# Projecting the S5 part of the second half's tiles before the feed-forward, with the last early tile's residual and norm in halves on VectorE

## The chip, the cores and the metric

One of the eight cores of one Trainium2 chip runs the whole program. The metric is device time in microseconds, the median of several executions of the same program. Everything is float32; matrix products run on operands split into a high and a low part (fp32r), three TensorE instructions for each product.

## What is computed

A decoder layer for 1024 positions of width 1024. The part that matters here is the output projection of the mixers and the second sub-layer (cut from the reference):

```python
mix = jnp.concatenate([rms_norm(o_a, out_norm_g[l, :a_end]),
                       rms_norm(o_b, out_norm_g[l, a_end:b_end]),
                       rms_norm(o_c, out_norm_g[l, b_end:])], axis=-1)
x = x + ga1 * (mix @ w_out[l])

h = rms_norm(x, norm2_g[l]) * (1 + sc2) + sh2
x = x + ga2 * (jnp.square(jax.nn.relu(h @ w_ff1[l])) @ w_ff2[l])
```

`o_a` (384 columns) comes from a sliding-window attention, `o_b` (256 columns) from the S5 state-space mixer, `o_c` (384 columns) from the three-branch attention. The rows of `w_out` are therefore eight slabs of 128: slabs 0 to 2 belong to A, 3 and 4 to S5, 5 to 7 to C.

## The kernel before

The 1024 positions are eight tiles of 128. S5 is finished for all tiles early (about a quarter into the span); its normed output lies in DRAM as `mixB_d`. Attention A and C go tile by tile. Tiles 0 to 3 (the first half) are finished first; then the feed-forward of the first half (`feed_forward`, L2153) runs while attention goes through tiles 4 to 7, then the output projection of the second half (`late_proj`, L1806) runs between the last pieces of that feed-forward, and last the feed-forward of the second half (`late_feed_forward`, L2118).

The output projection of one tile for one group of slabs is, for each of two column halves of 512, three TensorE instructions a slab (`mm3`, so 12 instructions of 128x512 a tile for the two S5 slabs, 18 for the three A or C slabs), and one addition into the tile's page `y[n]` (`add_y`, L1516). A and C need a factor of the norm for each row, so `add_y` scales them; S5 is normed before and needs none (`r is None`).

- `early_ab` (L1771) loads slabs 0 to 4, projects A and S5 of tiles 0 to 3 as soon as attention A has left them, then loads slabs 5 to 7 and the gate row `rows_of[2]`.
- `tile_end(n)` (L1792), for n of 0 to 3, projects C, adds the residual (`residual`, L1668: the gate on GpSimd, the addition on VectorE, over all 1024 columns), then the second norm and its transposition (`norm2_steps`, L1683): a square sum on ScalarE, the reciprocal root on GpSimd (`rstd_pool`, L470), the scaling on VectorE, and four `turn` steps of two TensorE transposes each. The first product of `feed_forward` needs tile 3's last `turn` steps.
- `late_proj` loads slabs 0 to 2, then 3 and 4, then 5 to 7, and projects the groups A, S5 and C of tiles 4 to 7 in this order, group after group.
- `load_ff` (L1905) loads a feed-forward weight slab of 512 KB, copies the high part on ScalarE and takes the low part on GpSimd.

The order of all instructions is not the order of the code. The code is run once to record calls; `run_plan` (L405) takes the steps by planned times, and `listed` (L216) then lists the recorded calls on the engines by the planned rank, readiness and its own prices. What comes out is a fixed order on each in-order engine. In the profile all recorded instructions have the line L2191, so groups are told apart by tile names: `pa` and `pb` are the eight banks of PSUM, `b` the pages of 1024, `u` those of up to 804, `s` of 384, `small` the columns of statistics, `wide` the identity of a transpose.

## Time and profile before

| | |
|---|---|
| median of 3 runs | 1365.98 us (1362.07 to 1370.18) |
| the profiled execution's own time | 1368.67 us |
| its span in the trace | 1367.0 us |
| mean granted TensorE clock | 0.973 |
| TensorE busy | 1306.1 us (96%) |
| VectorE busy | 954.8 us (70%) |
| ScalarE busy | 749.3 us (55%) |
| GpSimd busy | 639.1 us (47%) |

Shares of busy time are averages over stages that have different limits; the tables by stretch and the timelines below say what each stage is limited by. A granted clock of 1.00 is 2.4 GHz, of 0.50 is 1.2 GHz; a value between is a mean over a stretch that had both.

### The profile page before, as it was taken

What the parts mean: (1) busy time and instruction counts of PE and PEld (TensorE: products, weight loads), DVE (VectorE), ACT (ScalarE), POOL (GpSimd) and SP (SyncE); (2) the same over time, 40 slices, a digit from 0 to 9 for tenths busy, and PEclk for the clock granted to TensorE, in tenths of its full rate; (3) what the DMA queues carried; (4) which work ended last, traced back from release to release, by engine and by line L of the source; (5) the groups of instructions that cost most, each with busy time, mean ns of one, the idle gap of its engine ahead of it and who ended that gap; (6) DMA issues with size and microseconds to landing.
All of it is one profiled execution on the core that took longest, in us unless ns stands there. A gap on an engine that the chain in (4) does not pass through costs nothing.

```text
span 1367.0 us, 19734 instructions
## 1 busy us (share of the span) xinstructions
PE 1306.1 (96%) x6862; PEld 1115.3 (82%) x6862; DVE 954.8 (70%) x1979; ACT 749.3 (55%) x1657; POOL 639.1 (47%) x604
## 2 busy tenths in 40 slices
PE   5998998998999869999999999999999999999998
PEld 4898998997787558888888888888787888888886
DVE  7868977787788545465565576463558887788896
ACT  6445367567666775565565565542354445544450
POOL 3477734034567365455465465575553233122230
PEclk9999999999899789999999999999999999999999
DMA  9445436223122222212222343244464432323221
GB/s 364 177 141 170 153 117 214 95 72 116 39 76 108 89 89 69 74 64 68 95 80 62 119 144 120 75 143 146 153 223 162 155 123 78 107 94 108 78 93 62
DMA packets 59570, 161.03 MB, mean 118 GB/s; under 512 B 6447, under 2 KB 22349, under 8 KB 59469
## 3 DMA queue, kind: packets, MB, share of 16 engines
q1 hardware_dynamic: 51661, 145.86, 32.3%
q10 hardware_dynamic: 7808, 13.91, 2.7%
q8 instruction: 54, 0.88, 0.3%
q14 instruction: 47, 0.39, 0.1%
HBM read 140.59 MB, written 19.14 MB: 117 GB/s over the span
## 4 chain that ended last, share of the span: by engine, by line
PE 76%; DVE 7%; ACT 3%; issue 2%; POOL 1%; DMA 1%; ACTq 0%; DVEq 0%; SPq 0%; POOLq 0%
PE pb L2191 41%; PE pa L2191 35%; DVE b L2191 4%; ACT b L2191 2%; DVE pb L2191 1%; ACT u L2191 1%; POOL b L2191 1%; DMA mixB_d<-b 1%; DVE k L2191 1%; DVE small L2191 0%; DVE u L2191 0%; DVE s L2191 0%; DMA b<-in_ada_dram 0%; ACT s L2191 0%; ACT k L2191 0%
## 5 line engine op out<-in xcount | busy, mean ns | idle before, releaser
L2191 PE MATMUL pb<-b,b 128*128 128x512 f32 (+2 forms) x2478 | 590.2, 385 | 1.4 <-DVE b L2191 1.3
L2191 PEld LDWEIGHTS pb<-b,b 128*128 128x128 f32 (+1 forms) x2478 | 446.0, 190 | 85.7 <-DVE b L2191 2.8
L2191 POOL TENSOR_TENSOR b<-b,b 128x1024 fp32r<-128x1024 f32 (+6 forms) x140 | 322.7, 2312 | 293.2 <-ACT b L2191 188.0
L2191 PE MATMUL pa<-b,b 128*128 128x512 f32 (+2 forms) x1830 | 364.3, 349 | 9.5 <-ACT b L2191 4.4
L2191 PEld LDWEIGHTS pa<-b,b 128*128 128x128 f32 (+1 forms) x1830 | 291.7, 195 | 49.8 <-ACT b L2191 5.3
L2191 ACT ACTIVATE b<-b 128x1024 fp32r<-128x1024 f32 (+4 forms) x266 | 242.0, 927 | 100.8 <-DMA b<-in_ff_dram 42.6
L2191 DVE TENSOR_TENSOR b<-b,b 128x1024 fp32r<-128x1024 f32 (+4 forms) x181 | 200.2, 1136 | 21.8 <-ACT b L2191 12.1
L2191 PE MATMUL pa<-u,b 128*128 128x384 f32 (+2 forms) x836 | 202.0, 364 | 7.4 <-DVE small L2191 2.0
L2191 PEld LDWEIGHTS pa<-u,b 128*128 128x128 f32 x836 | 148.3, 206 | 16.2 <-ACT u L2191 4.6
L2191 DVE TENSOR_TENSOR b<-pa,b 128x512 f32<-128x512 f32 (+2 forms) x168 | 107.6, 650 | 65.3 <-PE pa L2191 61.8
L2191 ACT ACTIVATE u<-pa 128x384 fp32r<-128x384 f32 (+4 forms) x205 | 97.1, 478 | 84.3 <-PE pa L2191 83.3
L2191 DVE TENSOR_TENSOR u<-pa,u 128x384 fp32r<-128x384 f32 (+1 forms) x173 | 94.9, 553 | 55.7 <-ACT u L2191 55.2
L2191 DVE TENSOR_TENSOR b<-pb,b 128x512 f32<-128x512 f32 (+2 forms) x120 | 76.2, 647 | 60.1 <-PE pb L2191 55.2
L2191 POOL TENSOR_SCALAR b<-b,small 128x64 f32<-128x64 f32 (+8 forms) x118 | 75.2, 648 | 68.9 <-DVE small L2191 55.8
L2191 PE MATMUL pa<-wide,b 128*128 128x128 f32 (+1 forms) x443 | 81.7, 296 | 24.8 <-DVE b L2191 19.1
L2191 POOL TENSOR_SCALAR u<-u,small 128x256 f32<-128x256 f32 (+3 forms) x90 | 55.1, 623 | 100.0 <-DVE small L2191 78.4
L2191 PEld LDWEIGHTS pa<-wide,b 128*128 128x128 f32 (+1 forms) x443 | 58.4, 149 | 43.5 <-DVE b L2191 21.2
L2191 POOL TENSOR_TENSOR b<-r,b 128x512 fp32r<-128x512 f32 x37 | 51.2, 1383 | 80.6 <-ACT b L2191 80.1
L2191 ACT ACTIVATE b<-pb 128x512 f32<-128x512 f32 (+3 forms) x60 | 29.1, 509 | 87.0 <-PE pb L2191 72.4
L2191 ACT ACTIVATE u<-pb,small 128x256 f32<-128x256 f32 (+6 forms) x126 | 60.2, 485 | 28.7 <-DVE small L2191 28.0
L2191 ACT ACTIVATE b<-pb,small 128x64 f32<-128x64 f32 (+4 forms) x130 | 62.5, 493 | 20.4 <-DVE small L2191 15.6
L2191 PE MATMUL pb<-k,u 128*128 128x320 f32 (+10 forms) x300 | 70.0, 344 | 2.3 <-ACT b L2191 2.1
(145 smaller groups left out, 1446.2 us busy)
## 6 DMA issues: line engine op xcount, KB each, us to landing
b<-in_ff_dram SPq DMA_DIRECT2D x128, 512.0 KB, 3.6
b<-in_ada_dram SPq DMA_DIRECT2D x48, 512.0 KB, 6.0
b<-in_x_dram SPq DMA_DIRECT2D x16, 512.0 KB, 7.1
b<-in_wo_dram SPq DMA_DIRECT2D x16, 512.0 KB, 4.3
r<-in_w_in_dram SPq DMA_DIRECT2D x16, 256.0 KB, 2.6
b<-in_cw_dram SPq DMA_DIRECT2D x8, 512.0 KB, 5.4
x_d<-b ACTq DMA_DIRECT2D x8, 512.0 KB, 3.2
out_dram<-b SPq DMA_DIRECT2D x16, 256.0 KB, 2.2
```

What stands on the lines that cost most here:

```text
L2191: method(*args, **kw)
```

## The change

1. In `early_ab`, after the last slabs are loaded, the S5 group of tiles 4, 5 and 6 is projected and the pages go to a new DRAM tensor `yB_d`, through ScalarE's queue. Tile 7's is projected in `tile_end(3)`. `add_y` copies the first S5 half instead of scaling it.
2. `late_proj` has two groups of slabs, A and C. It loads the pages from `yB_d` on SyncE's queue and adds to them. The loads and splits of slabs 3 and 4, and the four loads of `mixB_d`, go from there.
3. For tile 3 alone `half_residual` takes the place of `residual`: gate and addition on VectorE in halves of 512 columns, each followed by its square sum on ScalarE; the norm adds the two sums on VectorE and scales in halves.
4. The low parts of the first four feed-forward weight slabs of the first half are taken on VectorE instead of GpSimd.

```diff
@@ add_y
-            ts(d, o, r, ALU.mult)
+            if r is None:
+                V.tensor_copy(out=d, in_=o)
+            else:
+                ts(d, o, r, ALU.mult)
@@ new
+    def half_residual(n, i):
+        c = slice(i * 512, i * 512 + 512)
+        if not i:
+            normed[n] = page(1024)
+        tt(y[n][:, c], y[n][:, c], rows_of[2][:, c], ALU.mult)
+        tt(x2[n][:, c], x2[n][:, c], y[n][:, c], ALU.add)
+        A.activation(out=normed[n][:, c], in_=x2[n][:, c], func=AF.Square, accum_out=ss4[:, i:i + 1])
+        if i:
+            nc.scalar.dma_start(out=x2_d[n], in_=x2[n])
@@ norm2_steps, scale
+            if t in normed:
+                h = normed[t]
+                tt(ss2[:, t:t + 1], ss4[:, 0:1], ss4[:, 1:2], ALU.add)
+                rstd_pool(rs2[:, t:t + 1], ss2[:, t:t + 1], 1, D)
+                for c in (slice(0, 512), slice(512, 1024)):
+                    ts(h[:, c], x2[t][:, c], rs2[:, t:t + 1], ALU.mult)
@@ early_ab, behind load_row(2)
+        for n in range(NT // 2, NT - 1):
+            steps = proj_steps(n, [3, 4], load_b(n))
+            for f in steps:
+                f()
+                yield 6.0 / len(steps)
+            nc.scalar.dma_start(out=yB_d[n - 4], in_=y.pop(n))
@@ tile_end
-        for f in proj_steps(n, [5, 6, 7], st) + [lambda: residual(n)] + norm2_steps(n):
+        steps = proj_steps(n, [5, 6, 7], st)
+        if n == 3:
+            for i in range(2):
+                steps.insert(2 * i + 1, lambda i=i: half_residual(n, i))
+            steps += proj_steps(7, [3, 4], load_b(7)) + [lambda: nc.scalar.dma_start(out=yB_d[3], in_=y.pop(7))]
+        else:
+            steps.append(lambda: residual(n))
+        steps += norm2_steps(n)
+        for f in steps:
@@ late_proj
-        late, tiles, groups = {}, range(4, NT), ((0, 1, 2), (3, 4), (5, 6, 7), ())
+        late, tiles, groups = {}, range(4, NT), ((0, 1, 2), (5, 6, 7), ())
-                if i == 1:
-                    late[n] = load_b(n)
-                    continue
+                if not i:
+                    y[n] = page(1024)
+                    nc.sync.dma_start(out=y[n], in_=yB_d[n - 4])
@@ load_ff
-        split_lo(G, lo, raw, hi)
+        split_lo(V if not half and kind == 1 and i < 4 else G, lo, raw, hi)
```

How the change moves instructions shows at three places.

TensorE, behind the C projection of tile 3 (the last product of it is the first row; `b314,u608` and `b314,u617` are score products of the next attention unit; `wide,b612` and `wide,b622` are tile 3's norm transposes; `b418,u620` to `b422,u620` are tile 7's S5 group; `u610` and `u621` are attention weights). Before:

```order
L2191 MATMUL pa2_65<-b548_629,b606_687 128x512
L2191 MATMUL pb0_67<-b314_395,u608_689 128x256 x4
L2191 MATMUL pb1_68<-b314_395,u608_689 128x256 x2
L2191 MATMUL pa1_64<-wide_91,b612_693 128x128
L2191 MATMUL pa2_65<-wide_91,b612_693 128x128
...
L2191 MATMUL pa1_64<-wide_91,u610_691 128x128 x3
L2191 MATMUL pa2_65<-wide_91,q611_692 128x128 x3
L2191 MATMUL pb2_69<-b571_652,b619_700 128x512
```

After:

```order
L2229 MATMUL pa2_65<-b548_630,b615_697 128x512
L2229 MATMUL pb0_67<-b314_396,u617_699 128x256 x3
L2229 MATMUL pb1_68<-b314_396,u617_699 128x256 x2
L2229 MATMUL pa1_64<-b418_500,u620_702 128x512
...
L2229 MATMUL pa2_65<-b422_504,u620_702 128x512
L2229 MATMUL pa1_64<-wide_91,u621_703 128x128 x3
L2229 MATMUL pa3_66<-u626_708,b275_357 128x384
L2229 MATMUL pa2_65<-wide_91,q623_705 128x128 x3
...
L2229 MATMUL pa2_65<-wide_91,b622_704 128x128
```

Twelve products of tile 7's S5 group, and then transposes, value and score products of the attention, stand between the score products and tile 3's transposes, where before nothing stood.

VectorE, the same place (`b517` is tile 3's page `y`, `b609` and `b618` its residual, `b612` and `b622` its normed page, `b624` tile 7's page, `b636` and `b639` low parts of feed-forward slabs). Before:

```order
L2191 SCALAR_TENSOR_TENSOR b517_598<-pa1_64,small_71,b517_598 128x512
L2191 SCALAR_TENSOR_TENSOR b517_598<-pa2_65,small_71,b517_598 128x512
L2191 ISA pb0_67,small_71<-pb0_67,u322_403,small_71 128x256
...
L2191 TENSOR_REDUCE small_71<-small_71 128x3
L2191 TENSOR_TENSOR b609_690<-b609_690,b517_598 128x1024
L2191 RECIPROCAL small_71<-small_71 128x3
L2191 TENSOR_SCALAR b612_693<-b609_690,small_71 128x1024
```

After:

```order
L2229 SCALAR_TENSOR_TENSOR b517_599<-pa1_64,small_71,b517_599 128x512
L2229 TENSOR_TENSOR b636_718<-b634_716,b635_717 128x1024
L2229 TENSOR_TENSOR b517_599<-b517_599,b556_638 128x512
L2229 SCALAR_TENSOR_TENSOR b517_599<-pa2_65,small_71,b517_599 128x512
L2229 TENSOR_TENSOR b618_700<-b618_700,b517_599 128x512
L2229 TENSOR_TENSOR b517_599<-b517_599,b556_638 128x512
L2229 COPY b624_706<-pa1_64 128x512
L2229 TENSOR_TENSOR b618_700<-b618_700,b517_599 128x512
...
L2229 COPY b624_706<-pa2_65 128x512
L2229 TENSOR_TENSOR u626_708<-pa1_64,u626_708 128x384
L2229 TENSOR_TENSOR small_71<-small_71 128x1
L2229 TENSOR_TENSOR b639_721<-b637_719,b638_720 128x1024
...
L2229 TENSOR_SCALAR b622_704<-b618_700,small_71 128x512
```

Gate, addition and scaling of tile 3 stand in halves on VectorE, with two low parts, the two copies of tile 7's page and attention splits between them; the rows left out are the score maxima, as before, and two more attention splits.

TensorE in the late projection, between the A group and the C group (`u1083`, `u1099` are the last A tile; in the first fence `u1099` of slabs `b1087` is the first S5 tile; `ones` are the norm sums of the C group; `u1114` is the first C tile). Before:

```order
L2191 MATMUL pa2_65<-b1071_1152,u1083_1164 128x512
L2191 MATMUL pb0_67<-b574_655,b1056_1137 128x512
...
L2191 MATMUL pa3_66<-b1087_1168,u1099_1180 128x512
...
L2191 MATMUL pb2_69<-b1094_1175,u1099_1180 128x512
L2191 MATMUL pb3_70<-b1060_1141,b1040_1121 128x512
```

After:

```order
L2229 MATMUL pa2_65<-b1081_1163,u1099_1181 128x512
L2229 MATMUL pb0_67<-b574_656,b1068_1150 128x512
...
L2229 MATMUL pa0_63<-ones_92,s1115_1197 128x1 x3
...
L2229 MATMUL pb0_67<-b576_658,b1069_1151 128x512
L2229 MATMUL pa1_64<-ones_92,s1124_1206 128x1 x3
L2229 MATMUL pa3_66<-b1102_1184,u1114_1196 128x512
```

Before, the S5 group follows the A group, in turn with feed-forward products; now the C group follows after one feed-forward unit's eighteen products and the four norm sums.

The S5 group of tile 4 now stands on both sides of the C projections of tiles 0 and 1, in two pieces of six products; those of tiles 5 and 6 stand further on among attention and norm transposes of tiles 1 to 3, in two pieces of six each as well.

## Rows read from the trace of the kernel before

**Rows 1.** The page, part 4: the chain that ended last, by engine.
```profile
PE 76%; DVE 7%; ACT 3%; issue 2%; POOL 1%; DMA 1%; ACTq 0%; DVEq 0%; SPq 0%; POOLq 0%
```

**Rows 2.** Busy time by stretch; columns: us, then busy us and count of each engine, granted clock.
```profile
900.00:1000.00 100.00, 99.42 (x473) 81.81 (x473) 54.87 (x75) 38.22 (x61) 58.14 (x49) 1.00 0.42 138
```

**Rows 3.** Busy time by stretch around the long gap, columns as in Rows 2.
```profile
429.80:441.00 11.20, 10.43 (x61) 8.70 (x60) 10.72 (x34) 8.40 (x28) 10.36 (x13) 1.00 0.39 141
441.00:456.00 15.00, 11.61 (x47) 6.44 (x45) 10.12 (x26) 14.57 (x41) 7.83 (x8) 0.80 0.21 72
456.00:472.20 16.20, 12.92 (x63) 9.84 (x63) 9.67 (x23) 11.48 (x27) 3.93 (x4) 0.82 0.14 45
472.20:479.70 7.50, 7.49 (x24) 5.91 (x24) 2.82 (x7) 1.94 (x8) 3.72 (x4) 0.66 0.67 199
...
489.20:500.00 10.80, 10.16 (x47) 8.29 (x48) 4.36 (x14) 9.24 (x24) 4.68 (x3) 0.76 0.37 116
```

**Rows 4.** Timeline of TensorE, 432 to 493 us: start, us, operation, [idle before <-releaser].
```profile
432.85 2.23 PE L2191 MATMUL pa<-b,b 128*128 128x512 f32 x9
...
472.18 6.80 PE L2191 MATMUL pa<-b,b 128*128 128x512 f32 x18 [0.54 <-ACT b L2191]
478.81 0.88 PE L2191 MATMUL pb<-b,u 128*128 128x256 f32 x6
489.21 0.69 PE L2191 MATMUL pa<-wide,b 128*128 128x128 f32 x2 [9.52 <-DVE b L2191]
...
492.52 1.20 PE L2191 MATMUL pb<-b,b 128*128 128x512 f32 x2
```

**Rows 5.** Timeline of VectorE, 479 to 489 us.
```profile
479.01 0.75 DVE L2191 SCALAR_TENSOR_TENSOR b<-pa,small,b 128x512 f32<-128x512 f32 x1 [1.77 <-PE pa L2191]
479.68 0.48 DVE L2191 CUSTOM_DVE_ANT_1 pb<-pb,u,small 128x256 f32<-128x256 f32 x1
...
482.90 1.23 DVE L2191 TENSOR_TENSOR b<-b,b 128x1024 f32<-128x1024 f32 x1
...
488.18 0.98 DVE L2191 TENSOR_SCALAR b<-b,small 128x1024 f32<-128x1024 f32 x1 [3.97 <-POOL small L2191]
```

**Rows 6.** Timeline of GpSimd, 479 to 489 us.
```profile
479.84 2.34 POOL L2191 TENSOR_TENSOR b<-b,b 128x1024 f32<-128x1024 f32 x1 [1.38 <-DVE b L2191]
483.81 2.52 POOL L2191 TENSOR_TENSOR b<-b,b 128x1024 fp32r<-128x1024 f32 x1 [1.62 <-ACT b L2191]
...
486.87 0.19 POOL L2191 TENSOR_SCALAR small<-small 128x1 f32<-128x1 f32 x1
...
487.60 0.55 POOL L2191 TENSOR_TENSOR small<-small 128x1 f32<-128x1 f32 x1
```

**Rows 7.** Timeline of TensorE, 932 to 954 us.
```profile
932.75 1.56 PE L2191 MATMUL pa<-b,u 128*128 128x512 f32 x6
934.15 1.57 PE L2191 MATMUL pb<-b,u 128*128 128x512 f32 x6
...
953.40 2.34 PE L2191 MATMUL pa<-b,u 128*128 128x512 f32 x9
```

**Rows 8.** Timelines of SyncE's queue and of GpSimd, 925 to 944 us.
```profile
925.31 5.89 SPq L2191 DMA_DIRECT2D b<-in_wo_dram  x3
...
936.21 7.14 POOL L2191 TENSOR_TENSOR b<-b,b 128x1024 fp32r<-128x1024 f32 x3
```

**Rows 9.** Groups of VectorE instructions by shape: count, busy us, mean ns, idle before.
```profile
L2191 DVE TENSOR_TENSOR u<-pa,u 128x384 fp32r<-128x384 f32 x157 | 86.2, 554 | 51.9 <-ACT u L2191 51.3
...
L2191 DVE COPY b<-pa 128x512 f32<-128x512 f32 x14 | 9.3, 687 | 7.7 <-issue 4.9 <-PE pa L2191 2.8
```

**Rows 10.** Timelines of VectorE and of GpSimd, 461 to 466 us.
```profile
461.60 0.41 DVE L2191 TENSOR_TENSOR b<-b,b 128x256 fp32r<-128x256 f32 x1
...
464.07 1.35 DVE L2191 TENSOR_TENSOR b<-b,b 128x256 fp32r<-128x256 f32 x1
...
462.77 2.37 POOL L2191 TENSOR_TENSOR b<-b,b 128x1024 fp32r<-128x1024 f32 x1 [10.76 <-ACT b L2191]
```

More of the change, by code (lines that the diff above doesn't have):

```diff
@@ L30 @@
 SLOTS = dict(k=(1088, 4), b=(1024, 38), u=(804, 10), r=(804, 2), s=(384, 5), q=(384, 1))
-SMALL = 1288
+SMALL = 1292
 TC = dict(schedule_with_timeline_sim=True)
@@ L1672, in residual @@
         nc.scalar.dma_start(out=x2_d[n], in_=x2[n])
+    normed = {}
+    def half_residual(n, i):
[7 more added lines that the diff above has]
+            nc.scalar.dma_start(out=x2_d[n], in_=x2[n])
     def load_row(v):
@@ L1680, in trunk @@
     h2l = [None, None]
-    ss2, rs2 = cols(8), cols(8)
+    ss2, rs2, ss4 = cols(8), cols(8), cols(3)
     def norm2_steps(t):
@@ L1690, in scale @@
                 h2l[hf] = [page(1024) for _ in range(4)]
-            h = page(1024)
-            A.activation(out=h, in_=x2[t], func=AF.Square, accum_out=ss2[:, t:t + 1])
-            rstd_pool(rs2[:, t:t + 1], ss2[:, t:t + 1], 1, D)
-            ts(h, x2[t], rs2[:, t:t + 1], ALU.mult)
+            if t in normed:
[5 more added lines that the diff above has]
+            else:
+                h = page(1024)
+                A.activation(out=h, in_=x2[t], func=AF.Square, accum_out=ss2[:, t:t + 1])
+                rstd_pool(rs2[:, t:t + 1], ss2[:, t:t + 1], 1, D)
+                ts(h, x2[t], rs2[:, t:t + 1], ALU.mult)
             hold.append(h)
@@ L1734, in trunk @@
     oC_d = dr.tile([4, 128, 384], F32, name="oC_d")
+    yB_d = dr.tile([4, 128, 1024], F32, name="yB_d")
     def a_phase():
@@ L1800, in tile_end @@
         load_x2(n)
-        for f in proj_steps(n, [5, 6, 7], st) + [lambda: residual(n)] + norm2_steps(n):
+        steps = proj_steps(n, [5, 6, 7], st)
[3 more added lines that the diff above has]
+            steps += proj_steps(7, [3, 4], load_b(7)) + [lambda: nc.scalar.dma_start(out=yB_d[3], in_=y.pop(7))]
+        else:
+            steps.append(lambda: residual(n))
+        steps += norm2_steps(n)
+        for f in steps:
             f()
@@ L1811, in late_proj @@
             yield L_PACE
-        for i, fs in enumerate(groups[:3]):
+        for i, fs in enumerate(groups[:2]):
             for n in tiles:
                 yield L_PACE
-                if i == 1:
-                    late[n] = load_b(n)
-                    continue
+                if not i:
+                    y[n] = page(1024)
+                    nc.sync.dma_start(out=y[n], in_=yB_d[n - 4])
                 o, late[n] = load_o(oC_d[n - 4] if i else oA_d[n]), []
```

## Prediction

> **What bounds the kernel now.** I read the chain of waits first: three quarters of it lie on TensorE, 7% on VectorE, little elsewhere [rows 1]. So the question for every part of the change is whether it takes TensorE work off a stretch where TensorE is full, or fills a stretch where it waits. The table of busy time by stretch answers that. From 500 us to the end of the late projection TensorE has next to no idle time: 99.42 us of the 100 from 900 to 1000, at the full clock [rows 2]. Around 430 to 500 us it looks otherwise: TensorE is busy 11.61 of 15.0 us and 12.92 of 16.2 us there, its granted clock is 0.80 and 0.82, and 0.66 in the last C projection [rows 3]. The timeline shows why the end of this stage is worst: after tile 3's C projection (18 products from 472.18) and six score products, TensorE does nothing for 9.52 us and then starts tile 3's transposes at 489.21; the first feed-forward product follows at 492.52 [rows 4]. What it waits for is a chain over three engines. VectorE adds the second half at 479.01 [rows 5]; GpSimd applies the gate, 2.34 us; VectorE adds the residual, 1.23 us; ScalarE sums squares; GpSimd is then busy with a feed-forward low part (2.52 us from 483.81) before it takes the root, 486.87 to 488.15 [rows 6]; VectorE scales from 488.18 [rows 5]. Everything behind 492.52 is TensorE at its limit, so a microsecond taken before that point, or a product taken out behind it, comes off the end.
>
> **Late projection: out.** The S5 group of tiles 4 to 7 is 4 tiles x 2 halves x 2 slabs x 3 = 48 products of 128x512. In the timeline, groups of six start 1.40 us apart (932.75, 934.15), 0.233 us a product [rows 7], so 48 x 0.233 = 11.2 us leave a full TensorE. VectorE's eight additions go with them, and two slab loads with their splits; TensorE does not wait for these there, so they count nothing. What may come back: slabs 5 to 7 are requested from 925.31 and GpSimd ends their low parts at 943.35 [rows 8], 18.0 us later, while the C group starts only at 953.40 [rows 7], with the S5 group between. In the new order only eighteen feed-forward products and the norm sums stand between A and C, about 4.2 + 1.4 us. If the request kept its distance to the A group's end (6 us before it), C would wait 12.0 - 5.6 = 6.4 us. On SyncE four page loads from `yB_d` are new ahead of these requests, four small ones from `mixB_d` and two slabs fewer. Bounds 0 and +6.4; in the listed order C products come before the rest of a feed-forward unit that could have gone first, so I am near zero: **+1.0**.
>
> **Early stretch: in.** Tiles 4 to 6 bring 36 products. Bounds: nothing, if they all fall into idle time, and 36 x 0.233 = 8.4 us if none does; the stretch from 429.8 to 472.2 has 7.4 us idle. Tile 4's twelve fall where TensorE is busy 10.43 of 11.20 us, VectorE 10.72 and GpSimd 10.36 [rows 3]; I count them in full, 2.8 us. The other 24 fall between 441 and 472, where TensorE has 6.7 us idle and a low clock, but ScalarE is busy 14.57 of 15.0 us. ScalarE gets a high-part copy for each tile and the issue of a store to `yB_d`. VectorE gets six copies of 0.69 us [rows 9] and three splits of 0.41 us (rows 10 have one of that width), 5.4 us in a stretch where it has 12. For these I take 1.2 us. Together **+4.0**, bounds 0 and about +10 (8.4 and the rest for ScalarE).
>
> **The gap.** From the start of tile 3's C projection to its transposes it is now 489.21 - 472.18 = 17.0 us. The new order makes VectorE the chain. With products at 0.233 us its queue goes: scale and add 0.75 (to 3.0 us), the low part of the first feed-forward slab 1.23 (4.3; priced as the residual addition of the same width), half a gate 0.62, scale and add 0.75, half an addition 0.62, half a gate 0.62, copy of tile 7's first half 0.69, half an addition 0.62 (8.2), three maxima at 0.48, the second copy 0.69, an attention split 0.55 [rows 9], the sum of the two square sums (11.0); then 1.28 us for the root on GpSimd, as in [rows 6], under a second low part and two more splits (13.3), and half a scaling 0.5: transposes at about 14.0 us, 3.0 earlier. With the products at the rate of the trace, 18 in 6.63 us or 0.37 each [rows 4], both copies wait for TensorE and the same queue gives about 17.2 us, +0.2. I take the middle, **-1.5**. Tile 7's twelve products (2.8 to 4.4 us) lie under this and cost nothing; were the gap to close without them, they would cost that.
>
> One more bound on this queue. At 464.07 a subtraction of 256 columns took 1.35 us on VectorE where another took 0.41 at 461.60; GpSimd's subtraction of 1024 columns ran from 462.77 to 465.14, and the slow one ended just behind it [rows 10]. Six instructions of the new queue (two low parts, four half gates and additions) are of that kind, both inputs in SBUF; if one of them meets a GpSimd subtraction of 2.5 us in full, the gap gets 2.5 us back. The first four feed-forward low parts leave GpSimd, so I leave it at zero and keep +2.5 as an end. The Trainium skill says the same in "SBUF — State Buffer", section "Who interferes with whom": a VectorE instruction with two SBUF inputs and a GpSimd instruction that reads SBUF block each other for the whole instruction. By that rule alone, moving the gate and low parts to VectorE would make the sum 2.5 us worse, and the slow subtraction agrees with it.
>
> **Work pulled ahead.** Between the C projection and the first feed-forward product now stand some 13 more attention instructions (value and score products, transposes) that came after it before; at 0.147 us each, six in 0.88 [rows 4], that is 1.9 us of later TensorE work. Part returns, because the first feed-forward unit has fewer fillers while it waits for the `turn` steps: **-1.0**, ends -1.9 and 0.
>
> **Sum:** -11.2 + 1.0 + 4.0 - 1.5 - 1.0 = **-8.7 us**. The profiled execution took 1368.67 us, so it would take 1360.0; the median of the runs shown is 2.7 us lower, and on it the forecast is 1365.98 - 8.7 = **1357.3 us**. About 0.5% (6.8 us) is what a measurement of this kernel can tell from no change.
>
> **The rivals.** *Forecast* as above, own range 1352 to 1361, chance 0.58.
>
> *A clock that stays high.* The granted clock is 0.66 to 0.82 from 441 us on, through and behind the gap [rows 3]. If the inserted products keep it at 2.4 GHz, the eighteen C products take 4.2 instead of 6.6 us and the chain takes the full -3.0; the early stretch costs +1.0, since what is there runs faster too; pulled-ahead work gives -1.9, and the stretch from 489.20 to 500, at 0.76, gives another 1: -11.2 + 1.0 + 1.0 - 3.0 - 1.9 - 1.0 = -15.1, or 1350.9 us. For it speaks the gap of 9.52 us that goes; against it, that the clock was already low at 441 to 472 without such a gap. Chance 0.18. The rule for it in the Trainium skill is in "TensorE: Matmul & The Clock Gate", section "What's actually happening": the low clock is the default and activity lifts it; by that rule the time would be this rival's, and the traces bear it out only in that the clock is 1.00 where TensorE is full.
>
> *The moved products cost the same early.* All 36 on the path (+8.4), no gain in the gap, nothing pulled ahead: -11.2 + 1.0 + 8.4 = -1.8, or 1364.2 us. For it: VectorE, GpSimd or ScalarE is full in two thirds of that stretch. Chance 0.16.
>
> *The late cover is missed:* C waits the 6.4 us for its slabs, 5.4 more than counted: -3.3, or 1362.7 us. Chance 0.05.
>
> *Slower: ScalarE held up by the stores to `yB_d`.* Three stores stand in ScalarE's in-order queue in the early stretch; each waits for VectorE's second copy, this for six products on TensorE. Behind a store wait the copies and `turn` steps of the attention and norm chains, on the engine that is busy 14.57 of 15.0 us [rows 3]. If a store holds ScalarE for t us, the early stretch costs 3t in place of 4.0: the sum is then -12.7 + 3t, and from t = 4.2 us the change is slower. The distance between a tile's first and second six products allows some 6.5 us: +6.8, or 1372.8 us. Against it: the order has the stores a few instructions behind the copies. Chance 0.03.
>
> **How the numbers follow.** The likeliest is 1357.3 us. Faster by over 0.5% (below 1359.2): 0.18 from the clock, about 0.43 of the forecast's 0.58, 0.01 of the rest, 0.62. Slower by over 0.5%: 0.02. Within: 0.36. The range runs from 1347, with most of the clock rival in, to 1365, with the early-cost and late-cover rivals in; outside are 0.05 below and 0.10 above.
>
> **What would show each step.** In the changed kernel's trace the late projection should have TensorE at 99% or more with the C group some 6 us behind the A group; a wait there over 3 us for a VectorE or GpSimd low part is the missed cover. From the start of tile 3's C projection (18 products) to its transposes there should be 14 to 17 us, with twelve products inside and no wait of TensorE near 9.52 us. The start of that projection should come 4 us later than 472.18; 8 us or more says that the moved products cost the same early. A clock of 1.00 there speaks for the clock rival, and a ScalarE that waits over 4 us before a `yB_d` store for the slow one. The forecast is wrong if the late products are gone and the time did not move.

## The result, and the profile after

The changed kernel takes 1353.46 us (median of 5 runs, 1353.26 to 1356.26); the kernel before took 1365.98 us beside it (1362.07 to 1370.21). The ratio is 0.9909, 95% interval 0.9883 to 0.9935, so 12.5 us are gone. The profiled execution took 1355.56 us with a span of 1353.8 us, against 1368.67 and 1367.0: 13.2 us less. The forecast was 1357.3 us with a range of 1347 to 1365: the direction and the main term were right, and the gain was half as large again.

The page of the changed kernel, part 1 and the chain of part 4: the shares hardly move against [rows 1], as the work moved within the same engines.

```profile
PE 1302.0 (96%) x6862; PEld 1111.5 (82%) x6862; DVE 957.4 (71%) x1988; ACT 748.1 (55%) x1657; POOL 631.3 (47%) x597
...
PE 76%; DVE 7%; ACT 3%; DMA 1%; issue 1%; POOL 1%; ACTq 0%; SPq 0%; DVEq 0%; POOLq 0%
```

Busy time by stretch in the changed kernel, with the limits and columns of [rows 2, 3] (us; busy us and count of PE, PEld, DVE, ACT, POOL; granted clock; DMA share; GB/s):

```profile
429.80:441.00 11.20, 11.20 (x69) 10.04 (x68) 10.43 (x34) 7.00 (x22) 9.54 (x11) 1.00 0.35 141
441.00:456.00 15.00, 12.62 (x56) 8.48 (x55) 11.06 (x28) 13.64 (x40) 8.38 (x10) 0.92 0.09 37
456.00:472.20 16.20, 14.70 (x77) 10.10 (x75) 11.15 (x23) 11.25 (x29) 0.00 (x0) 0.96 0.34 124
472.20:479.70 7.50, 6.46 (x26) 5.04 (x27) 3.80 (x13) 4.20 (x13) 2.96 (x6) 0.77 0.56 205
479.70:489.20 9.50, 7.81 (x38) 5.94 (x37) 9.50 (x22) 6.16 (x18) 1.65 (x2) 0.93 0.75 252
489.20:500.00 10.80, 9.95 (x35) 7.30 (x35) 6.64 (x24) 9.45 (x29) 5.01 (x6) 0.59 0.28 96
900.00:1000.00 100.00, 98.48 (x465) 80.69 (x465) 45.98 (x64) 39.10 (x59) 64.09 (x51) 1.00 0.44 150
```

Three readings. The early stretch took the new products into idle time, and its granted clock rose from 0.80 and 0.82 [rows 3] to 0.92 and 0.96. In the gap (479.7 to 489.2) TensorE is busy 7.81 us, and VectorE all of the 9.50: it is the chain there. And from 900 to 1000 us TensorE waits 1.52 us where it waited 0.58 [rows 2].

TensorE's timeline through the gap, to be held against [rows 4]:

```profile
474.46 1.22 PE L2229 MATMUL pa<-b,b 128*128 128x512 f32 x2 [0.87 <-ACT b L2229]
...
475.76 4.70 PE L2229 MATMUL pa<-b,b 128*128 128x512 f32 x16
480.30 0.75 PE L2229 MATMUL pb<-b,u 128*128 128x256 f32 x5
480.89 2.96 PE L2229 MATMUL pa<-b,u 128*128 128x512 f32 x12
...
485.61 0.44 PE L2229 MATMUL pa<-u,b 128*128 128x384 f32 x1 [1.43 <-ACT u L2229]
...
489.48 0.63 PE L2229 MATMUL pa<-wide,b 128*128 128x128 f32 x2
...
492.44 0.79 PE L2229 MATMUL pb<-b,b 128*128 128x512 f32 x1
```

Tile 3's C projection starts 2.28 us later than before (474.46 against 472.18), tile 7's twelve products follow it, and the wait of 9.52 us is gone; the longest is 1.43 us. The transposes start at 489.48, nearly when they did before (489.21), and the first feed-forward product at 492.44 (492.52 before). So up to this product nothing was won in time, but much more work is done.

VectorE's timeline there, to be held against [rows 5]:

```profile
478.51 0.75 DVE L2229 SCALAR_TENSOR_TENSOR b<-pa,small,b 128x512 f32<-128x512 f32 x1 [2.13 <-PE pa L2229]
479.18 1.81 DVE L2229 TENSOR_TENSOR b<-b,b 128x1024 fp32r<-128x1024 f32 x2
480.92 0.74 DVE L2229 SCALAR_TENSOR_TENSOR b<-pa,small,b 128x512 f32<-128x512 f32 x1
481.58 1.28 DVE L2229 TENSOR_TENSOR b<-b,b 128x512 f32<-128x512 f32 x2
...
486.32 1.21 DVE L2229 TENSOR_TENSOR b<-b,b 128x1024 fp32r<-128x1024 f32 x1
...
487.99 0.54 DVE L2229 TENSOR_TENSOR u<-pa,u 128x384 fp32r<-128x384 f32 x1
488.45 0.47 DVE L2229 TENSOR_SCALAR b<-b,small 128x512 f32<-128x512 f32 x1
```

From 478.51 to the half scaling at 488.45 this queue has no wait. GpSimd, which in [rows 6] had the gate, a low part and the root, now has only the root:

```profile
486.49 1.10 POOL L2229 TENSOR_SCALAR small<-small 128x1 f32<-128x1 f32 x1 [8.55 <-DVE small L2229]
487.67 0.55 POOL L2229 TENSOR_TENSOR small<-small 128x1 f32<-128x1 f32 x1
```

It idles 8.55 us before. Its first instruction takes 1.10 us where the same one took 0.19 [rows 6], and lies beside VectorE's low part of 486.32 to 487.53. The root still ends at 488.22, before VectorE has finished the attention split of 487.99 that stands ahead of the scaling; so this delay held nothing up.

In the late projection the last A products stand at 923.32 and the C group follows at 932.17, with no S5 group between ([rows 7] had it from 932.75, and C at 953.40):

```profile
923.32 2.26 PE L2229 MATMUL pa<-b,u 128*128 128x512 f32 x9
...
932.17 2.31 PE L2229 MATMUL pa<-b,u 128*128 128x512 f32 x9
```

**Where the time went.** One cut serves this and all experiments. Before any kernel here differs from another in TensorE's order, six column sums for a norm run; in both profiles they start at 397.70 us. From them to the start of tile 3's C projection is one stretch, from there to the first feed-forward product the second, from there to the last output stores (SyncE's queue, 1351.65 us before and 1338.55 after) the third. The sums and stores, before and after:

```profile
397.70 0.72 PE L2191 MATMUL pa<-ones,s 128*128 128x1 f32 x6
1351.65 12.57 SPq L2191 DMA_DIRECT2D out_dram<-b  x8
```

```profile
397.70 0.72 PE L2229 MATMUL pa<-ones,s 128*128 128x1 f32 x6
1338.55 12.57 SPq L2229 DMA_DIRECT2D out_dram<-b  x8
```

Busy time in the three stretches and their sum, before:

```profile
397.70:472.18 74.48, 65.98 (x341) 51.05 (x339) 56.03 (x165) 56.41 (x160) 45.04 (x50) 0.92 0.26 87
472.18:492.52 20.34, 10.19 (x35) 7.77 (x35) 7.16 (x18) 9.62 (x28) 13.44 (x12) 0.67 0.41 139
492.52:1351.65 859.13, 854.96 (x4062) 708.88 (x4061) 580.05 (x1051) 445.10 (x856) 389.55 (x262) 1.00 0.32 106
...
397.70:1351.65 953.95, 931.14 (x4434) 767.71 (x4433) 643.24 (x1232) 511.13 (x1042) 448.02 (x324) 0.98 0.32 106
```

and after:

```profile
397.70:474.46 76.76, 71.43 (x377) 55.24 (x375) 59.99 (x175) 56.34 (x164) 41.10 (x49) 0.98 0.30 104
474.46:492.44 17.98, 15.44 (x59) 11.13 (x59) 15.19 (x36) 11.51 (x32) 4.43 (x8) 0.78 0.73 256
492.44:1338.55 846.11, 841.45 (x4000) 698.74 (x4000) 569.87 (x1032) 442.01 (x848) 395.02 (x260) 1.00 0.32 108
...
397.70:1338.55 940.85, 928.31 (x4434) 765.11 (x4433) 645.05 (x1241) 509.86 (x1042) 440.54 (x317) 0.99 0.33 110
```

The three stretches change by +2.28, -2.36 and -13.02 us: -13.10 in all. TensorE has 4434 instructions in both. Its idle time (length less busy time) falls from 22.81 to 12.54 us, and its busy time by 2.83 us, with the clock up from 0.92 to 0.98 and from 0.67 to 0.78 in the first two stretches. So of the 13.1 us some 10.3 are waits that were filled; the other 2.8 I put down to the higher clock, as nothing was taken off TensorE's list. Of these 2.8, 0.8 lie in tile 3's C projection alone: from its first product to the score products behind it, it took 6.63 us before (472.18 to 478.81) and 5.84 after (474.46 to 480.30).

### The profile page after: what moved, and what is told of

Read it like the earlier page. It is cut to its first block, busy times and chain, and to the rows that moved or that the text cites. A ratio compares the mean times of both kernels' runs of the same rounds, so it can differ in the third digit from the quotient of the medians.

```text
span 1353.8 us, 19782 instructions
## 1 busy us (share of the span) xinstructions
PE 1302.0 (96%) x6862; PEld 1111.5 (82%) x6862; DVE 957.4 (71%) x1988; ACT 748.1 (55%) x1657; POOL 631.3 (47%) x597
## 4 chain that ended last, share of the span: by engine, by line
PE 76%; DVE 7%; ACT 3%; DMA 1%; issue 1%; POOL 1%; ACTq 0%; SPq 0%; DVEq 0%; POOLq 0%
PE pb L2229 41%; PE pa L2229 35%; DVE b L2229 5%; ACT b L2229 2%; POOL b L2229 1%; ACT u L2229 1%; DMA mixB_d<-b 1%; DVE pb L2229 0%; DVE k L2229 0%; DVE small L2229 0%; DMA b<-in_cw_dram 0%; DVE u L2229 0%; DMA b<-in_ada_dram 0%; ACT s L2229 0%; DMA out_dram<-b 0%
## 5 line engine op out<-in xcount | busy, mean ns | idle before, releaser
L2229 POOL TENSOR_TENSOR b<-b,b 128x1024 fp32r<-128x1024 f32 (+6 forms) x133 | 310.8, 2344 | 261.7 <-ACT b L2229 186.8
L2229 DVE TENSOR_TENSOR b<-b,b 128x1024 fp32r<-128x1024 f32 (+4 forms) x188 | 206.7, 1130 | 17.4 <-ACT b L2229 8.7
L2229 DVE TENSOR_TENSOR b<-pa,b 128x512 f32<-128x512 f32 (+2 forms) x164 | 104.7, 649 | 64.8 <-PE pa L2229 61.6
L2229 POOL TENSOR_SCALAR u<-u,small 128x256 f32<-128x256 f32 (+3 forms) x90 | 58.4, 660 | 123.4 <-DVE small L2229 89.0
L2229 DVE TENSOR_TENSOR b<-pb,b 128x512 f32<-128x512 f32 (+2 forms) x116 | 73.4, 645 | 54.9 <-PE pb L2229 49.7
L2229 PE MATMUL pa<-wide,b 128*128 128x128 f32 (+1 forms) x443 | 78.7, 290 | 15.5 <-DVE b L2229 9.9
```

What stands on the lines that cost most here:

```text
L2229: method(*args, **kw)
```

## The experiments

Times are medians, with ratios to the kernel before, run beside them. Beside them stands the cut, in us of each profiled execution: where the six sums start, the three stretches, their sum, TensorE's idle time in it, and the sum against before's 953.95.

| kernel | median (runs) | ratio, 95% interval | sums at | 1st | 2nd | 3rd | sum | idle | against before |
|---|---|---|---|---|---|---|---|---|---|
| before | | | 397.70 | 74.48 | 20.34 | 859.13 | 953.95 | 22.81 | |
| changed | 1353.46 (5) | 0.9909, 0.9883 to 0.9935 | 397.70 | 76.76 | 17.98 | 846.11 | 940.85 | 12.54 | -13.10 |
| changed again | 1353.83 (6) | 0.9904, 0.9868 to 0.9940 | 398.81 | 76.73 | 18.04 | 846.09 | 940.86 | 12.61 | -13.09 |
| e1 late group out | 1355.13 (6) | 0.9904, 0.9885 to 0.9922 | 395.28 | 74.65 | 19.55 | 847.71 | 941.91 | 22.64 | -12.04 |
| e2 no early group | 1356.31 (6) | 0.9908, 0.9889 to 0.9926 | 399.65 | 73.81 | 17.20 | 849.80 | 940.81 | 19.47 | -13.14 |
| e5 halves, low parts only | 1360.71 (8) | 0.9945, 0.9924 to 0.9966 | 397.42 | 73.86 | 17.20 | 859.33 | 950.39 | 18.54 | -3.56 |
| e7 S5 move only | 1356.95 (10) | 0.9933, 0.9910 to 0.9955 | 392.19 | 77.02 | 22.98 | 846.65 | 946.65 | 15.83 | -7.30 |
| e3 low parts on GpSimd | 1358.28 (12) | 0.9931, 0.9907 to 0.9955 | 393.23 | 77.03 | 21.16 | 848.35 | 946.54 | 14.91 | -7.41 |
| e4 whole residual | 1358.54 (10) | 0.9929, 0.9903 to 0.9955 | 398.20 | 77.03 | 20.34 | 846.72 | 944.09 | 13.47 | -9.86 |
| e6 tile 7 early too | 1356.42 (6) | 0.9903, 0.9882 to 0.9924 | 398.56 | 76.04 | 16.59 | 849.21 | 941.84 | 16.78 | -12.11 |
| e10 two low parts | 1354.41 (7) | 0.9913, 0.9883 to 0.9944 | 393.62 | 76.81 | 17.96 | 846.84 | 941.61 | 13.10 | -12.34 |
| e8 copies on ScalarE | 1355.34 (6) | 0.9909, 0.9876 to 0.9942 | 390.39 | 76.90 | 17.99 | 845.48 | 940.37 | 13.07 | -13.58 |
| e8 again | 1353.81 (7) | 0.9907, 0.9875 to 0.9939 | 395.63 | 76.94 | 17.96 | 846.27 | 941.17 | 13.84 | -12.78 |
| e9 early group twice | 1358.80 (10) | 0.9934, 0.9913 to 0.9954 | 397.73 | 77.95 | 19.64 | 845.95 | 943.54 | 11.97 | -10.41 |

The whole times of most variants can't be told apart by their intervals. One reason is in the fourth column: the sums start anywhere from 390.39 to 399.65 us, behind the same TensorE instructions. The cut leaves that out: two profiles of the changed kernel give 940.85 and 940.86, two of e8 940.37 and 941.17. I read differences over 1 us from it, and none below; each variant but these two has one profile.

One difference in the cut is larger than that and lies ahead of what the edits change on TensorE. Up to the end of tile 3's C projection TensorE's list is the same in the changed kernel, e3, e4, e7, e8 and e10. From its first product to the score products behind it that projection took 5.81 to 5.87 us in both profiles of the changed kernel and in e10, at a granted clock of 0.72 to 0.74, but 7.10 in e3 and e7, 7.15 in e4, 7.28 and 7.26 in e8, at 0.57 to 0.59. The lists of before and e1 are also the same up to there: 6.63 at 0.61 and 5.83 at 0.71. e2 took 7.00 and e5 7.01, at 0.57. What decides the clock there is not shown: the two kernels with two profiles met the same one both times, so the edits may have a hand in it through other engines. About 1.3 us of a comparison between two rows may be this; below, the comparisons stand with it and without it.

### The late group left out, and the early group left out

e1 is the kernel before without the late S5 group; e2 is the changed kernel without the early one.

```diff
 e1, late_proj of the kernel before
-        late, tiles, groups = {}, range(4, NT), ((0, 1, 2), (3, 4), (5, 6, 7), ())
+        late, tiles, groups = {}, range(4, NT), ((0, 1, 2), (5, 6, 7), ())
-        for i, fs in enumerate(groups[:3]):
+        for i, fs in enumerate(groups[:2]):
-                if i == 1:
-                    late[n] = load_b(n)
-                    continue
 e2, early_ab, tile_end and late_proj of the changed kernel
-        for n in range(NT // 2, NT - 1):
-            steps = proj_steps(n, [3, 4], load_b(n))
...
-            steps += proj_steps(7, [3, 4], load_b(7)) + [lambda: nc.scalar.dma_start(out=yB_d[3], in_=y.pop(7))]
-                if not i:
-                    y[n] = page(1024)
-                    nc.sync.dma_start(out=y[n], in_=yB_d[n - 4])
```

> The kernel before, with the S5 group of tiles 4 to 7 left out of the late projection and put nowhere (the second half's projection lacks its S5 part; slabs 3 and 4 are not loaded a second time). It measures the late term alone. Theory: 48 products of 0.233 us leave a full TensorE and nothing comes back: 11.2 us less than the kernel before, TensorE without a wait over 1 us between the A and the C group. Rival (the cover is missed): the C group waits for slabs 5 to 7, and only 5 to 8 us go.

> The changed kernel, with the S5 products of tiles 4 to 7, their stores and their loads left out (the second half's projection lacks its S5 part). It measures what the 48 products cost in their new place. Theory: tile 3's C projection starts about 2.3 us earlier than in the changed kernel, and its transposes another 1 to 2 us, since the two copies of tile 7's page are gone from VectorE's queue: 3 to 4 us less than the changed kernel in all, so about 1350 us. Rival (they cost early as much as late): 11 us less, about 1342 us. Rival (they are free): the same time as the changed kernel.

The third stretch of e1:

```profile
489.48:1337.19 847.71, 843.62 (x4014) 699.80 (x4013) 568.98 (x1039) 441.30 (x850) 393.02 (x260) 1.00 0.32 106
```

Against before it is 11.42 us shorter: 11.34 of busy time, 0.08 of waits. That is the late term by itself, 48 products at 0.236 us, as the theory said. The 0.79 us that its second stretch is shorter are the clock of the C projection. The wait before the transposes stays (9.53 us), so the gap is untouched by it.

e2 has 48 products less than the changed kernel and takes as long (940.81 against 940.85): my theory of 3 to 4 us less missed, and the early products cost nothing in sum. They bring 6.97 us more busy time (928.31 less 921.34) and take 6.93 us of waits away (19.47 to 12.54). They are not free where they stand: up to the first feed-forward product they cost 3.73 us (94.74 against 91.01 in the first two stretches). The third stretch gives 3.69 back, since the list of e2 has less of the later work pulled ahead (2.66 us more busy time behind that product) and waits 1.03 us more. And e2's C projection met the lower clock; at the changed kernel's 5.84 us the price would be 1.2 us, not 0.04.

### The halves and low parts without the move, and the move without them

e5 keeps the S5 group late and takes the third and fourth part of the change; e7 takes the first two parts alone (residual whole, low parts on GpSimd).

```diff
 e5, against the changed kernel: early_ab and tile_end without the S5 steps, late_proj as before
-        for n in range(NT // 2, NT - 1):
-            steps = proj_steps(n, [3, 4], load_b(n))
...
+        late, tiles, groups = {}, range(4, NT), ((0, 1, 2), (3, 4), (5, 6, 7), ())
 e7, against the changed kernel
-            for i in range(2):
-                steps.insert(2 * i + 1, lambda i=i: half_residual(n, i))
+            steps.append(lambda: residual(n))
-        split_lo(V if not half and kind == 1 and i < 4 else G, lo, raw, hi)
+        split_lo(G, lo, raw, hi)
```

> The kernel before with only the halves of tile 3's residual and norm and the four low parts on VectorE; the S5 group stays late. Theory: the gap has no TensorE work to hide, and VectorE's queue lacks the two copies: tile 3's transposes come 14 to 15 us after the start of its C projection in place of 17.0, and the time falls by 2 to 4 us, a long wait of 6 to 7 us of TensorE being left. Rival (the gap is ruled by something else, such as the norm's root): no change in the gap and in the time.

> The kernel before with the S5 part alone of the change: early projection and late loads; residual and norm whole, all low parts on GpSimd. Theory: the late term of 11.2 us and what the early stretch costs (2.3 us) give 8 to 10 us against the kernel before, and the gap stays near 17 us from the start of tile 3's C projection to its transposes, with tile 7's twelve products in it; the rest of the changed kernel's gain (2 to 4 us) is the halves and the low parts. Rival: the whole gain of 12 to 13 us is there without them.

Alone, the halves and low parts give 3.56 us, within the 2 to 4 expected, with the transposes 13.77 us behind the start of the C projection (14 to 15 expected); the longest wait, though, was 2.20 us and not 6 to 7, as the list pulled attention work into it. The move alone gives 7.30, less than the 8 to 10 expected, and its gap is 19.72 us, not 17. Together they give 13.10, or 2.2 us more than the two apart. Most of that is the clock of the C projection: at 5.84 us in all four, the parts would give 3.9 and 7.8 of 12.3, and 0.6 would be left, less than the cut can tell. Likewise the early products cost 946.65 - 941.91 = 4.74 us from e1 to e7 (no halves), 3.5 with the clock taken out, against the 1.2 above. So that one part needs the other is not shown beyond that. What e7 pays in the second stretch, 22.98 us, is seen in GpSimd's timeline:

```profile
477.35 2.41 POOL L2228 TENSOR_TENSOR b<-b,b 128x1024 f32<-128x1024 f32 x1 [2.31 <-DVE b L2228]
481.33 2.38 POOL L2228 TENSOR_TENSOR b<-b,b 128x1024 fp32r<-128x1024 f32 x1 [1.58 <-ACT b L2228]
...
485.44 0.55 POOL L2228 TENSOR_TENSOR small<-small 128x1 f32<-128x1 f32 x1
```

and VectorE's:

```profile
487.25 0.16 DVE L2228 TENSOR_REDUCE small<-small 128x1 f32<-128x2 f32 x1 [1.51 <-ACT u L2228]
...
487.64 1.23 DVE L2228 TENSOR_SCALAR b<-b,small 128x1024 f32<-128x1024 f32 x1
```

The gate (2.41 us) and a low part (2.38 us) lie ahead of the root, as before. Then the root is ready at 485.99, but the scaling starts only at 487.64: VectorE, in order, waits 1.51 us for ScalarE in an attention step that the list put ahead of it. That is a wait the pulled-in attention brought.

### Each of the two helpers taken back

e3 puts the four low parts back on GpSimd; e4 takes the whole residual and norm for tile 3 and leaves the low parts on VectorE.

```diff
 e3
-        split_lo(V if not half and kind == 1 and i < 4 else G, lo, raw, hi)
+        split_lo(G, lo, raw, hi)
 e4
-            for i in range(2):
-                steps.insert(2 * i + 1, lambda i=i: half_residual(n, i))
+            steps.append(lambda: residual(n))
```

> The changed kernel with the low parts of the first four feed-forward slabs back on GpSimd. Theory (VectorE's queue rules the gap, and GpSimd is idle there from 478 to 486 us): two low parts of about 1.2 us leave VectorE's queue before tile 3's scaling, its transposes come 1 to 2.4 us earlier, and the time falls by 1 to 2 us against the changed kernel. Rival (the two engines block each other): GpSimd's subtractions of 2.4 us stand against the half gates and additions, or in front of the root, and the transposes come 1 to 3 us later.

> The changed kernel with tile 3's residual and norm whole again (gate on GpSimd, one addition, one square sum, one scaling); the S5 products stay where the change put them, tile 7's behind the C projection. Theory: the chain behind the second half of the C projection gets the gate of 2.3 us, the addition of 1.2, the square sum of 1.2, the root of 1.3 and the scaling of 1.0 one after the other, 7.5 to 8.5 us to the transposes, where the changed kernel takes 8.7 from its second scale-and-add to the transposes: the same within 1.5 us, since halves on VectorE only trade the gate on GpSimd for a longer VectorE queue. Rival (the halves are what closes the gap): 3 us or more slower.

> The changed kernel again, beside its variants on one chip: 1353 to 1356 us.

The second stretch takes 21.16 us in e3 and 20.34 in e4, against 17.98 (and 18.04 when the changed kernel ran again, unedited, beside them). Over the whole cut e3 loses 5.7 us and e4 3.2; without the 1.3 us of the C projection's clock, 4.4 and 1.9. So in e3 the theory missed and the rival came, and e4 lies between its theory and its rival. From the score products to the transposes e3 takes 11.14 us (488.50 - 477.36) and the changed kernel 9.18. Why is in the rows of VectorE, GpSimd and TensorE:

```profile
471.56 5.96 PE L2229 MATMUL pa<-b,b 128*128 128x512 f32 x16
...
478.63 1.89 DVE L2229 TENSOR_TENSOR b<-b,b 128x512 f32<-128x512 f32 x3
480.44 2.84 DVE L2229 TENSOR_TENSOR b<-b,b 128x512 f32<-128x512 f32 x1
...
480.13 2.60 POOL L2229 TENSOR_TENSOR b<-b,b 128x1024 fp32r<-128x1024 f32 x1 [4.05 <-ACT b L2229]
...
484.03 0.87 PE L2229 MATMUL pa<-wide,u 128*128 128x128 f32 x3 [3.13 <-DVE b L2229]
```

Of the four half gates and additions three take 1.89 us together, 0.63 each, as the two of the changed kernel do (1.28 us for both). The fourth takes 2.84 us, 480.44 to 483.28: GpSimd's low part had begun at 480.13 and runs to 482.73. So some 2.2 us are lost in one instruction, about the 1.96 us by which the gap is longer, and TensorE waits 3.13 us behind it. This is the collision of [rows 10] at a place where it counts. The Trainium skill ("SBUF — State Buffer", section "Who interferes with whom") says that a VectorE instruction with two SBUF inputs contends with a GpSimd instruction that reads SBUF, and that the shared ports are an exclusive lock. The trace agrees: the one that came second, at 480.44, ended 0.55 us after the other was done. The change avoids this by leaving GpSimd nothing long to do there. The remaining 2.2 us of e3, in its third stretch, are not explained. e4 has such a meeting too, later: VectorE's third low part took 3.38 us from 492.91, beside GpSimd's of 2.81 us from 492.41.

### How many low parts, and where tile 7 goes

```diff
 e10
-        split_lo(V if not half and kind == 1 and i < 4 else G, lo, raw, hi)
+        split_lo(V if not half and kind == 1 and i < 2 else G, lo, raw, hi)
 e6
-        for n in range(NT // 2, NT - 1):
+        for n in range(NT // 2, NT):
-            steps += proj_steps(7, [3, 4], load_b(7)) + [lambda: nc.scalar.dma_start(out=yB_d[3], in_=y.pop(7))]
```

> The changed kernel, but only the first two low parts of feed-forward slabs are on VectorE, the third and fourth back on GpSimd. If the run with all four on GpSimd lost its 5 us because GpSimd has low parts ahead of the root of tile 3's norm, then the first two are the ones that count and this kernel takes 1353 to 1354.5, with a third and fourth that GpSimd takes behind the root. If GpSimd's long subtractions hold up VectorE's instructions wherever they lie together (the shared port), half of the loss returns: about 1356.

> The changed kernel with tile 7's S5 products put with those of tiles 4 to 6, so that none stands beside tile 3's residual and norm. Theory: in the early stretch 36 products cost 2.3 us, so 12 more cost about 1 us; the copies leave VectorE's queue in the gap, which gets 1 to 1.4 us shorter: within 1.5 us of the changed kernel, with a TensorE wait of 3 to 5 us in the gap again. Rival (the place in the gap is what pays): 2.8 us or more slower than the changed kernel.

e10's second stretch is 17.96 us, the changed kernel's 17.98, and its time is as its theory had it: the first two low parts are the ones that count, and the others may stay on GpSimd. In e6 tile 7's group goes early. The gap is then the shortest of all (16.59 us), but TensorE waits in it again (3.32 us in one piece), and the third stretch is 3.1 us longer. In sum it is 1.0 us behind the changed kernel, as expected and at the edge of what the cut can tell.

### VectorE's queue in the gap

```diff
 e8, add_y
             if r is None:
-                V.tensor_copy(out=d, in_=o)
+                if n == 7:
+                    A.activation(out=d, in_=o, func=AF.Copy)
+                else:
+                    V.tensor_copy(out=d, in_=o)
```

> The changed kernel, but the two copies of tile 7's S5 page from PSUM (0.69 us each on VectorE) go to ScalarE, which waits 5.4 us in this gap. If VectorE's queue alone sets the start of tile 3's transposes, the distance from the start of tile 3's C projection to the transposes falls from 15.0 by about 1.4 us (13.6), and the time is about 1 us shorter than the changed kernel's 1353.5 (1352 to 1353). If something else sets it (TensorE's own work of 12 products and the attention pulled into the gap), the distance shortens by under 0.5 us and the time stays within 1 us of it.

> The kernel with tile 7's copies on ScalarE once more. Counted from the six column sums of tile 1's norm near 395 us to the last output stores, its first profile took 940.37 us and the changed kernel's two profiles 940.85 and 940.86. If the 0.5 us are its own, this profile gives 940.0 to 940.6, whenever the sums start; if they came from the clock in that execution, 940.8 or more. The time as a whole will again say little: the start of those sums alone has varied from 390 to 400 us between profiles of the same instructions.

Miss and half a hit. From the C projection's start to the transposes it took 14.95 us (482.24 - 467.29), not 13.6. But the projection itself ran slower, its last sixteen products 6.13 us against 4.70:

```profile
467.29 1.22 PE L2232 MATMUL pa<-b,b 128*128 128x512 f32 x2 [0.87 <-ACT b L2232]
...
468.60 6.13 PE L2232 MATMUL pa<-b,b 128*128 128x512 f32 x16
474.57 0.76 PE L2232 MATMUL pb<-b,u 128*128 128x256 f32 x5
...
482.24 0.33 PE L2232 MATMUL pa<-wide,b 128*128 128x128 f32 x1
```

From the score products behind it to the transposes the changed kernel takes 489.48 - 480.30 = 9.18 us, e8 7.67 (482.24 - 474.57), and again 7.66. So VectorE's queue does set the gap, and 1.5 us came off with two copies; the slower products gave it back, in both profiles. The move of the copies is not needed for that: the same sixteen took 5.96 us in e3 and e7 and 6.01 in e4, where the copies stay. In time e8 is the same as the changed kernel: 940.37 and 941.17 in the cut around 940.85, so the 0.5 us of its first profile were not its own.

### The early group twice

```diff
 e9, early_ab
-            steps = proj_steps(n, [3, 4], load_b(n))
-            for f in steps:
-                f()
-                yield 6.0 / len(steps)
+            mb = load_b(n)
+            for k in range(2):
+                fresh[n] = set()
+                for f in proj_steps(n, [3, 4], mb):
+                    if n not in y:
+                        y[n] = page(1024)
+                    f()
+                    yield 3.0
```

> The changed kernel, but the S5 group of tiles 4, 5 and 6 is projected twice in the early stretch, the second result overwriting the first: 36 more products, six more copies on VectorE. Theory (the early stretch has idle TensorE time, and a low clock that more products raise): the products go in at 0 to 0.06 us each, and from the six column sums of tile 2 near 430 us to the start of tile 3's C projection it takes 44.3 to 46.5 us in place of 44.3; time 1353 to 1356. Rival (the first 36 already used the idle time up): 0.23 us each, 52 us in that stretch, time about 1361.

Thirty-six more products cost 943.54 - 940.85 = 2.69 us, 0.075 each where a late one costs 0.236 (e1). From the column sums near 430 us to the start of the C projection it took 45.53 us (430.15 to 475.68), as the theory had it; the median of 1358.80 lies between its 1353 to 1356 and the rival's 1361. TensorE's idle time falls by only 0.57 us more, to 11.97: the rest is the clock. The second stretch:

```profile
475.68:495.32 19.64, 17.57 (x80) 13.44 (x81) 15.73 (x38) 13.10 (x37) 6.80 (x10) 1.00 0.68 234
```

Its granted clock is 1.00, with 80 instructions in 17.57 us busy; the changed kernel has 0.78, with 59 in 15.44. Over the cut TensorE's busy time grows by 3.26 us, for 36 products worth 8.4 at the full clock. In e2, without any early products, it is 0.70 here. With the same early products it lies between 0.70 (e3) and 0.84 (e4), so the value of a single profile is no exact measure; but 1.00 is the highest of all.

## Why the prediction was right, and by how much it was off

Term by term, profiled execution against profiled execution:

| term | forecast | measured | from |
|---|---|---|---|
| late group out | -11.2 | -11.3 | e1, busy time of the third stretch |
| given back late | +1.0 | +0.5 | idle of the third stretch, 4.17 to 4.66 |
| early stretch | +4.0 | +2.3 | start of tile 3's C projection, 472.18 to 474.46 |
| the gap | -1.5 | -2.0 | from there to the transposes, 17.03 to 15.02 |
| transposes to the first product | none | -0.3 | 3.31 to 2.96 |
| work pulled ahead | -1.0 | -2.2 | busy time of the third stretch, -13.51, less the late group's -11.34 |
| sum | -8.7 | -13.1 | |

**Late group.** Right, and so was the reason: TensorE is the bound there at the full clock, and a product taken out is 0.236 us (e1).

**Given back.** The missed cover did not come: C follows the last A products without a long wait. What the term stood for is there in small: 0.94 us more idle time from 900 to 1000 us, against 0.37 less from 500 to 900. TensorE is busy 98.48 of these 100 us, a little under the 99% named as the sign. The most telling comparison is e1, with 0.16 us idle from 900 to 1000: the late projection can close up, but the list of the changed kernel doesn't do it. Which instruction is late there was not tried.

**Early stretch.** The term that was mis-sized most is the price of tiles 4 to 6: 2.8 us for tile 4 "in full" and 1.2 for the others. It was sized by idle time at the clock of before. The measured 2.3 (3.0 from e2 to the changed kernel, 76.76 against 73.81) lies between the forecast's 4.0 and the 1.0 of the rival with a clock that stays high: the clock rose to 0.92 and 0.96, and TensorE's busy time there grew by 5.45 us for 36 products worth 8.4. e9 shows the direction most plainly (36 more products, 8.4 us of work, 2.7 us of time), and e2 the other way (456 to 472 us at 0.80 without them). The rest of that rival did not come: the C projection's last sixteen products still took 4.70 us, and 489.2 to 500 us ran at 0.59, lower than the 0.76 of [rows 3].

```profile
456.00:472.00 16.00, 13.18 (x64) 9.90 (x64) 10.59 (x24) 12.09 (x28) 0.73 (x1) 0.80 0.14 45
```

(e2; the changed kernel's row is above.)

**The gap.** VectorE became the chain, as the new order said: it was busy without a break, the first scale-and-add at 478.51, the half scaling 9.94 us later. The distance to the transposes, 15.02 us, lies between the two bounds of 14.0 and 17.2 that I averaged to 15.5. That the term came out so near is in part luck. Of the 2.01 us, 0.79 are the C projection at a higher clock than in before's profile, and other profiles of the same list have it slower than before (e3, e4, e7, e8); the queue's own part is 10.40 to 9.18 us behind it, 1.22. The port term was put at zero with an end of +2.5, and zero it was: GpSimd's first root instruction took 1.10 in place of 0.19 beside a low part on VectorE, but VectorE came to the scaling later than the root was done. The sentence that by the rule alone of the Trainium skill ("SBUF — State Buffer", the same section) moving the gate and the low parts would make the sum 2.5 us worse had the wrong sign for the low parts: with them on GpSimd the collision is there (e3, 2.2 us), with them on VectorE nothing on the path to the transposes is held by one.

**Work pulled ahead.** I let half of 1.9 us return, since the first feed-forward units would lack fillers. Nothing returned: from 500 to 900 us TensorE is idle 0.00 us at two digits in the changed kernel, 0.37 before. This is the largest miss beside the early stretch.

**The rivals.** Slower by the stores to `yB_d`: ScalarE's queue issues those of the early stretch at 434.98, 458.53 and 470.32 and tile 7's at 485.90, 0.33 us each, and the engine sits idle at none of them for over 0.3 us. Refuted. The moved products cost the same early: refuted with the whole change in place, and partly true without the halves and low parts, where e7 pays 4.7 us (3.5 without the C projection's clock) for 48 products. The late cover missed: refuted.

What stays open: why e2 has 1.6 us more idle time in its third stretch than e1 (5.69 against 4.09), though the late parts of both have the same work; what decides which clock the C projection meets; and where e3 loses the 2.2 us of its third stretch.

## What to carry to other kernels

Work taken from a stretch where the bound engine is full, and put where it waits on others, is worth its full price there (11.3 us here) and costs less in its new place; shortening the chain that causes the waits adds its own part. Each half of this change gave less alone (3.6 and 7.3 us of 13.1). Moving long two-input work from GpSimd to VectorE paid here because GpSimd was then left with nothing long to collide with: ask what both engines do at that time, not either alone. To compare variants that differ by 1 to 5 us, cut the profiles at a landmark ahead of which the instructions are the same; whole times hid what the cuts showed. Then compare the granted clock stretch by stretch as well: a stretch with the same list differed by up to 1.5 us from it.

## What the runs showed of the hardware that was not expected

- The same TensorE instructions ahead of the landmark took 390.39 us in e8 and 399.65 us in e2. Where they started late the granted clock was 0.93 in each of the first two stretches of 102 us; in e8 it was 0.98 and 0.97:

```profile
0.00:102.00 102.00, 85.00 (x499) 76.84 (x499) 74.38 (x185) 51.30 (x89) 51.66 (x113) 0.93 0.62 227
102.00:204.00 102.00, 96.67 (x644) 93.35 (x643) 86.85 (x128) 54.81 (x134) 62.77 (x45) 0.93 0.45 147
```

(the changed kernel, sums at 397.70) and

```profile
0.00:102.00 102.00, 84.16 (x510) 75.07 (x511) 75.48 (x188) 52.71 (x93) 54.34 (x114) 0.98 0.64 232
102.00:204.00 102.00, 97.24 (x666) 93.98 (x664) 91.62 (x137) 59.38 (x150) 61.50 (x45) 0.97 0.49 160
```

(e8, sums at 390.39). TensorE is busy for much the same time in both and gets further. That alone is as much as most variants differ by.

- Added products can pay for most of themselves: 36 of them raised TensorE's busy time by 3.26 us instead of 8.4, as the clock from the C projection to the first feed-forward product went from 0.78 to 1.00 (e9, one profile).
- A one-column GpSimd instruction took 1.10 us in place of 0.19 beside a VectorE subtraction of 1.21 us, and a VectorE instruction of 512 columns took 2.84 in place of 0.68 beside a GpSimd subtraction of 2.60 us (e3): the collision hits short instructions as much as long ones, on either side.
